# Seven block products for eight in the gated branch and the output projection, over all 1024 tokens

## Chip, cores and metric

The kernel runs on one core of one Trainium2 chip. The metric is the device time of one launch in microseconds; the median of three runs counts. Everything is float32.

## What is computed

One decoder layer on x (1 x 1024 x 2048), then a final modulated norm:

```python
mod = c_act @ w_ada + b_ada                  # shift, scale, gate
h = modulate(rms_norm(x, norm_g), shift, scale)
proj = h @ w_in                              # 2048 x 5632
u_a, v_a, z_a, q, k, v, z_b = split(proj)    # 1024, 1024, 1024, 1024, 256, 256, 1024
y_a = chunked_spatial_gating(u_a, v_a, ...)  # u * (W_s LN(v) + b), chunks of 128 tokens
y_b = sliding_window_sink_attention(rope(q), rope(k), v, sinks)   # window 128
y = concat([y_a * silu(z_a), y_b * silu(z_b)])
x = x + gate * (y @ w_out)                   # 2048 x 2048
out = modulate(rms_norm(x, final_norm_g), shift_f, scale_f)
```

## The kernel before

The tokens are worked in two halves of 512. Every large product is taken in float32 accuracy from three matmuls on rounded operands: an operand is split into a high part (a copy on ScalarE, rounded) and a low part (the rest, a subtraction on VectorE or GpSimd), and `mm3` (L199) sums high x high, high x low, low x high in PSUM. `split_w` (L138) splits weights as they come; h is split once per half and kept in SBUF as 16 pairs of 128x512 tiles (`Hh`, `Hl`, one pair per 128 rows of the contraction, called kt).

`project` (L250) makes one group of 512 output columns: 16 steps (kt), each with four 128x512 outputs, so 16 x 4 x 3 = 192 matmuls of 512 columns. There are eleven groups: u0, u1, kv, q0, q1, va0, va1, zb0, zb1, za0, za1. The order of half 0 is: va0 and va1 on the unnormalised x, while `mod_col` (L155) makes the scale column; kv and q0 while it makes the shift column and `build_h` (L494) makes h; then `half` (L744): q1, zb0, zb1, u0, u1, za0, za1, and the output projection `out_phase` (L543). Half 1 builds its h during the end of half 0's output projection and runs kv, q0, q1, va0, va1, zb0, zb1, u0, u1, za0, za1 and the output projection.

Beside the projections run three kinds of work. `side` holds generators (attention, then the spatial sums of the gating branch); `tick` (L230) lets them advance by `credit` steps per kt. `bg` holds column work: `mod_col` takes two loads of 128x1024 of w_ada and two multiply-reduces on VectorE per column of 128 values (gate, final scale and shift: 96 of them), and `corr_bg` 16 similar blocks; `background(n)` advances it by n, and `background(1000)` empties it. The order on each engine is set by a scheduler when the kernel is built: program order with priorities (`tc.high_priority`). All loads and stores but one go through SyncE's queue, in order.

```python
mm3(o, lh, ll, rh, rl)    # o += lh.T rh + lh.T rl + ll.T rh
```

## Time and profile before

| what | us |
|---|---|
| runs, median (lowest to highest of 3) | 1536.05 (1533.2 to 1536.28) |
| profiled execution, span | 1539.1 |
| TensorE busy | 1461.2 (95%) |
| VectorE busy | 1000.6 (65%) |
| ScalarE busy | 630.8 (41%) |
| GpSimd busy | 253.6 (16%) |

The profiled execution is one execution of its own; the profile gives its span, 0.2% above the median of the runs, and no other time for it. A busy share is an average over stages; a row of matmuls gives their modelled length, while the distance between their starts is what one costs.

### The profile page before, as it was taken

How to read it: one execution, taken by the hardware profiler on the slowest of the kernel's cores; microseconds unless marked ns; L12 is line 12 of the kernel's file. 1: busy time of each engine (PE TensorE's matmuls, PEld its weight loads, DVE VectorE, ACT ScalarE, POOL GpSimd, SP SyncE). 2: the span in 40 equal slices, each digit the busy share in tenths (PEclk: the TensorE clock that was granted, in tenths of full speed). 3: DMA queues.
4: the chain of work that ended last, by engine and by line, in shares of the span. 5: the costliest groups of instructions: out<-in, count | busy, mean ns of one | idle time of the engine just before them, and what ended most of it. 6: DMA issues, size and time to landing. Idle time of an engine off the chain costs nothing.

```text
span 1539.1 us, 20360 instructions
## 1 busy us (share of the span) xinstructions
PE 1461.2 (95%) x7057; PEld 1213.1 (79%) x7057; DVE 1000.6 (65%) x1952; ACT 630.8 (41%) x1397; POOL 253.6 (16%) x183
## 2 busy tenths in 40 slices
...
GB/s 348 282 203 267 270 190 140 153 175 195 109 111 121 198 200 219 205 220 187 144 184 244 181 195 157 123 125 141 120 186 175 205 203 196 171 219 197 133 87 110
DMA packets 88106, 280.65 MB, mean 182 GB/s; under 512 B 12017, under 2 KB 12609, under 8 KB 88002
## 3 DMA queue, kind: packets, MB, share of 16 engines
...
q10 hardware_dynamic: 144, 0.52, 0.1%
...
## 4 chain that ended last, share of the span: by engine, by line
PE 43%; issue 28%; DVE 14%; DMA 9%; ACT 2%; POOL 2%; SPq 0%; DVEq 0%; ACTq 0%; POOLq 0%
PE mm L200 11%; PE mm L202 11%; PE mm L201 11%; DMA ring<-ada 4%; DVE ring L165 3%; DMA wr<-ada 1%; PE att L202 1%; PE att L201 1%; PE att L200 1%; DVE wl L149 1%; PE att L349 1%; DVE ring L720 1%; DVE y L165 1%; DMA ring<-wvaT 1%; DVE t L333 1%
## 5 line engine op out<-in xcount | busy, mean ns | idle before, releaser
L202 PE MATMUL mm<-r,wl 128*128 128x512 f32 x1024 | 403.5, 394 | 4.9 <-DVE wl L149 3.8
L200 PE MATMUL mm<-r,wh 128*128 128x512 f32 x1024 | 405.5, 396 | 0.8 <-ACT wh L148 0.4
L201 PE MATMUL mm<-r,wh 128*128 128x512 f32 x1024 | 403.4, 394 | 0.0
L148 ACT ACTIVATE wh<-wr 128x512 fp32r<-128x512 f32 x318 | 197.6, 627 | 335.5 <-PE mm L201 192.0
L149 DVE TENSOR_TENSOR wl<-wr,wh 128x512 fp32r<-128x512 f32 x226 | 163.8, 729 | 132.6 <-ACT wh L148 127.4
L202 PEld LDWEIGHTS mm<-r,wl 128*128 128x128 f32 x1024 | 194.5, 190 | 49.1 <-DVE wl L149 6.8
L200 PEld LDWEIGHTS mm<-r,wh 128*128 128x128 f32 x1024 | 195.3, 191 | 40.5 <-ACT y L279 1.2
L201 PEld LDWEIGHTS mm<-r,wh 128*128 128x128 f32 x1024 | 195.0, 190 | 37.8
L200 PE MATMUL mm<-wh,r 128*128 128x512 f32 (+1 forms) x448 | 171.4, 383 | 18.3 <-ACT r L656 16.0
L201 PE MATMUL mm<-wl,r 128*128 128x512 f32 (+1 forms) x448 | 170.9, 381 | 3.1 <-POOL wl L149 2.5
L148 ACT ACTIVATE wh<-ring 128x512 fp32r<-128x512 f32 x138 | 86.8, 629 | 207.7 <-PE mm L201 124.7
L149 POOL TENSOR_TENSOR wl<-wr,wh 128x512 fp32r<-128x512 f32 x92 | 130.5, 1420 | 228.4 <-ACT wh L148 209.7
L202 PE MATMUL mm<-wh,r 128*128 128x512 f32 (+1 forms) x448 | 166.7, 379 | 0.1
L201 PE MATMUL att<-wl,r 128*128 128x512 f32 (+1 forms) x448 | 161.7, 361 | 2.0 <-DVE wl L149 1.9
L200 PE MATMUL att<-wh,r 128*128 128x512 f32 (+1 forms) x448 | 161.0, 359 | 0.0
L202 PE MATMUL att<-wh,r 128*128 128x512 f32 (+1 forms) x448 | 161.0, 359 | 0.0
L149 DVE TENSOR_TENSOR wl<-ring,wh 128x512 fp32r<-128x512 f32 x138 | 97.7, 711 | 95.7 <-ACT wh L148 87.9
L200 PEld LDWEIGHTS mm<-wh,r 128*128 128x128 f32 x448 | 85.6, 191 | 38.5 <-ACT r L656 21.0
L474 POOL TENSOR_TENSOR y<-y,t 128x512 f32<-128x512 f32 x32 | 47.7, 1515 | 394.1 <-ACT t L483 349.3
L201 PEld LDWEIGHTS mm<-wl,r 128*128 128x128 f32 x448 | 85.8, 191 | 20.7 <-POOL wl L149 5.4
L201 PEld LDWEIGHTS att<-wl,r 128*128 128x128 f32 x448 | 84.7, 189 | 18.1 <-DVE wl L149 4.6
L202 PEld LDWEIGHTS mm<-wh,r 128*128 128x128 f32 x448 | 85.5, 191 | 16.0 <-DVE r L657 0.8
(213 smaller groups left out, 2033.4 us busy)
## 6 DMA issues: line engine op xcount, KB each, us to landing
wr<-win SPq DMA_DIRECT2D x124, 512.0 KB, 4.2
ring<-ada SPq DMA_DIRECT2D x90, 512.0 KB, 5.2
wr<-ada SPq DMA_DIRECT2D x55, 512.0 KB, 4.4
ring<-win SPq DMA_DIRECT2D x46, 512.0 KB, 3.9
wr<-wout SPq DMA_DIRECT2D x38, 512.0 KB, 3.6
ring<-wout SPq DMA_DIRECT2D x26, 512.0 KB, 3.9
ring<-wvaT SPq DMA_DIRECT2D x16, 512.0 KB, 5.3
y<-xn SPq DMA_DIRECT2D x16, 512.0 KB, 4.8
```

Of the source, the lines that this page charges most:

```text
L148: act.activation(R(w_hi[i]), r[:, kk, :], AF.Copy)
L149: (pool if on_pool else dve).tensor_tensor(R(w_lo[i]), r[:, kk, :], w_hi[i], op=ALU.subtract)
L165: dve.tensor_tensor_reduce(w, w, cb[:, c0:c0 + n], scale=1.0, scalar=prev, op0=ALU.mult, op1=ALU.add, accum_out=o)
L200: pe.matmul(o, lhsT=lh, rhs=rh, start=first, stop=False)
L201: pe.matmul(o, lhsT=lh, rhs=rl, start=False, stop=False)
L202: pe.matmul(o, lhsT=ll, rhs=rh, start=False, stop=last)
L333: dve.tensor_tensor_reduce(ps[i], os[i], mk, scale=-0.125, scalar=nsnk[:, h0 + i:h0 + i + 1], op0=ALU.add, op1=ALU.min, accum_out=nm[:, i: ...
L349: pe.transpose(pt_bank[:, c:c + P], p[:, 256 * i + P * j:256 * i + P * j + P], ident)
L474: pool.tensor_tensor(y, y, zz[c], op=ALU.mult)
L720: dve.tensor_tensor_reduce(ti, ti, misc, scale=1.0, scalar=prev, op0=ALU.mult, op1=ALU.add, accum_out=acc_)
```

## The change

u, za and the output projection leave `half`. They become eight *units* behind both halves: u, za, and the two column halves o0 and o1 of the output projection, each twice (c = 0, 1: the two halves of the contraction). A unit multiplies a 1024 x 1024 block of tokens and features by a 1024 x 1024 block of weights, both cut in 2 x 2, with seven products of 512 x 512 x 512 instead of eight. One product is 48 matmuls of 512 columns. For that the tokens' side needs seven operands (`SUMS`: blocks, sums and differences), built by `op_make` from h or y in DRAM and split in high and low; the weights' side needs four sums, made on GpSimd (`w_sums` and two more in `unit`). Results are added on VectorE from PSUM, and a first visit (c = 0) leaves its four partial results in DRAM (`part_d`) for the second.

h, y, v, the gating sums and u therefore go through DRAM (`h_d`, `y_d`, `v_d`, `s_d`, `us_d`). va of both halves comes first, one group over all 1024 tokens at a time (eight PSUM banks); weights of va are read once. The scale loop now holds va0, the shift loop va1, and kv and q0 follow alone. Half 1 does q0 before kv. Buffers come from three pools (`Arena`): `al2` gives 128x1024, `al` half of one, first free first.

```diff
+    def al2(self):
+        if not self.big:
+            raise MemoryError(f"{len(self.half)} halves left")
+        return self.big.popleft()
+
+    def al(self):
+        if not self.half:
+            self.half.extend(self.of[id(self.al2())][1])
+        return self.half.popleft()
+
+    def fr(self, t):
+        b, other = self.of[id(t)]
+        if b is t:
+            self.big.append(t)
+        elif any(x is other for x in self.half):
+            self.half = deque(x for x in self.half if x is not other)
+            self.big.append(b)
+        else:
+            self.half.append(t)
...
+    lend(both, 2, "w", NW)
+    lend(both, 1, "r", NR)
+    lend(both, 0, "f", NF)
+    front_r = lend(front, 1, "fr", NB - NW - NR - NF)
+    cb = [al2(), al2()]
...
+    def build_h(h, kt, rb):
+        x, hi, lo = al(), al(1), al(1)
+        sp.dma_start(out=x, in_=A["xT"][h, kt])
+        dve.scalar_tensor_tensor(x, x, scale_c[:, kt:kt + 1], rb, op0=ALU.mult, op1=ALU.mult)
+        act.activation(x, x, AF.Identity, bias=shift_c[:, kt:kt + 1])
+        sp.dma_start(out=h_d[h, kt], in_=x)
+        act.activation(R(hi), x, AF.Copy)
+        dve.tensor_tensor(R(lo), x, hi, op=ALU.subtract)
+        fr(x)
+        H[kt] = hi, lo
...
+    def w_load(u, b):
+        name, c = u
+        wts[b] = [al2() for _ in range(2)]
+        for jj in range(2):
+            sp.dma_start(out=two(wts[b][jj]), in_=A["ww"][PAIRS.index(name), c, BLOCKS.index(b), jj])
+
+    def w_sums():
+        wts["t2"] = [al2() for _ in range(2)]
+        for jj in range(2):
+            t3, t2 = wts["12"][jj], wts["t2"][jj]
+            pool.tensor_tensor(t3, wts["22"][jj], t3, op=ALU.subtract)
+            pool.tensor_tensor(t2, t3, wts["11"][jj], op=ALU.add)
+
+    def product(op, w, bank, feature, refill, first):
+        for jj in range(2):
+            hi, lo = al2(2), al2(2)
+            act.activation(R(hi), wts[w][jj], AF.Copy)
+            dve.tensor_tensor(R(lo), wts[w][jj], hi, op=ALU.subtract)
+            ah, al_ = ops[op][jj]
+            for i in range(2):
+                for s in range(4):
+                    n, m = slice(512 * i, 512 * i + 512), slice(512 * i + s * P, 512 * i + s * P + P)
+                    x, y = ((hi, lo), (ah, al_)) if feature else ((ah, al_), (hi, lo))
+                    mm3(bank[s], R(x[0])[:, m], R(x[1])[:, m], R(y[0])[:, n], R(y[1])[:, n],
+                        first and jj + i == 0, jj + i == 2, not first)
+            fr(hi, lo)
+        while stale:
+            op_make(*stale.pop())
+        if refill:
+            stale.append((op, *refill))
...
+    SUMS = {"11": ["11"], "s2": ["21", "22", "-11"], "12": ["12"], "s3": ["11", "-21"], "s1": ["21", "22"], "22": ["22"],
+            "s4": ["12", "11", "-21", "-22"]}
+
+    def op_make(name, src, kind, c):
+        if name in ops:
+            for t in ops.pop(name):
+                fr(*t)
+        made = []
+        for jj in range(2):
+            total = None
+            for b in SUMS[name]:
+                t = al2()
+                rows_ = ROWS[kind][c][int(b[-1]) - 1]
+                sp.dma_start(out=two(t), in_=src[int(b[-2]) - 1, rows_[2 * jj]:rows_[2 * jj] + 2].rearrange("k p t -> p k t"))
+                if total is None:
+                    total = t
+                else:
+                    dve.tensor_tensor(total, total, t, op=ALU.subtract if b[0] == "-" else ALU.add)
+                    fr(t)
+            hi, lo = al2(1), al2(1)
+            act.activation(R(hi), total, AF.Copy)
+            dve.tensor_tensor(R(lo), total, hi, op=ALU.subtract)
+            fr(total)
+            made.append((hi, lo))
+        ops[name] = made
...
+        w_load(u, "21")
+        product("11", "11", X, feature, refill, True)
+        p1 = [al() for _ in range(4)]
+        evac(lambda s: act.activation(p1[s], X[s], AF.Copy))
+        for jj in range(2):
+            pool.tensor_tensor(wts["11"][jj], wts["22"][jj], wts["t2"][jj], op=ALU.subtract)
+        if c:
+            u2, u3, c21 = past(1), past(3), past(2)
+            for t in (u2, u3, c21):
+                for s in range(4):
+                    pool.tensor_tensor(t[s], t[s], p1[s], op=ALU.add)
+            fr(*p1)
+            c11 = past(0)
+        hk(0)
+        product("s2", "t2", Y, feature, refill, True)
+        if c == 0:
+            u2 = [al() for _ in range(4)]
+            add(u2, Y, p1)
         else:
...
+            add(u2, Y, u2)
+        hk(1)
+        product("12", "21", X, feature, refill, False)
...
+            add(c11, X, c11)
+        leave(0, c11)
+        for jj in range(2):
+            pool.tensor_tensor(wts["21"][jj], wts["21"][jj], wts["t2"][jj], op=ALU.subtract)
+        fr(*wts.pop("t2"))
+        hk(2)
+        product("s3", "12", Y, feature, refill, False)
+        if c == 0:
+            u3 = [al() for _ in range(4)]
+            add(u3, Y, p1)
+        else:
+            add(u3, Y, u3)
+        fr(*wts.pop("12"))
+        w11 = wts.pop("11")
+        if nxt:
+            w_load(nxt, "11")
+        n11 = wts.pop("11", None)
+        wts["11"] = w11
+        hk(3)
+        product("s1", "11", X, feature, refill, True)
+        add(u3, X, u3)
+        leave(3, u3)
+        fr(*wts.pop("11"))
...
+            wts["11"] = n11
+            w_load(nxt, "12")
...
+        product("22", "21", Y, feature, refill, False)
...
+        add(c21, Y, c21)
+        leave(2, c21)
+        fr(*wts.pop("21"))
+        w22 = wts.pop("22")
+        if nxt:
+            w_load(nxt, "22")
...
+    for kt in range(KT):
...
+        a = scale_c[:, kt:kt + 1]
+        for _ in mod_col("scale", kt, a):
             pass
...
+        if kt % 2 == 0:
+            wr = chunk(A["win"][GI["va0"], kt // 2])
         dve.tensor_tensor(a, a, cols[:, C_G + kt:C_G + kt + 1], op=ALU.mult)
-        act.activation(R(Hh[kt]), X[kt], AF.Copy, scale=a)
-        dve.scalar_tensor_tensor(R(Hl[kt]), X[kt], a, Hh[kt], op0=ALU.mult, op1=ALU.subtract)
-        if kt == 0:
-            act.activation(acc, X[kt], AF.Square)
-        else:
-            q = sq[kt % 2]
-            act.activation(q, X[kt], AF.Square)
-            pool.tensor_tensor(acc, acc, q, op=ALU.add)
-
-    vb = project(["va0", "va1"], ["mm", "att"], per_kt=g1_kt, pool_lo=("va0",),
-                 steps=[(kt, g) for kt in range(KT - 2) for g in ("va0", "va1")]
-                 + [(kt, g) for g in ("va0", "va1") for kt in (KT - 2, KT - 1)])
-    raws, rings = deque(w_raw), deque(ring)
-
...
+        for h in range(2):
+            x, hi, lo = al(), al(1), al(1)
+            sp.dma_start(out=x, in_=A["xT"][h, kt])
+            act.activation(R(hi), x, AF.Copy, scale=a)
+            dve.scalar_tensor_tensor(R(lo), x, a, hi, op0=ALU.mult, op1=ALU.subtract)
+            XA[h, kt] = hi, lo
+            if kt == 0:
+                act.activation(acc[h], x, AF.Square)
+            else:
+                q = al()
+                act.activation(q, x, AF.Square)
+                pool.tensor_tensor(acc[h], acc[h], q, op=ALU.add)
+                fr(q)
+            fr(x)
+        W = split_w(halves(wr)[kt % 2], on_pool=True)
+        if kt % 2:
+            fr(wr)
+        for T in range(8):
+            va_mm(T, kt, W)
+        fr(*W)
+
...
+    order = [(kt, T) for kt in range(2) for T in range(2, 8)] + ["spread"] + [(kt, T) for kt in range(2) for T in range(2)]
+    order += [(kt, T) for kt in range(2, KT) for T in range(8)]
...
+        kt, T = step
+        if kt not in va1:
+            for _ in mod_col("shift", kt, shift_c[:, kt:kt + 1]):
+                pass
+            if kt % 2 == 0:
+                wr = chunk(A["win"][GI["va1"], kt // 2])
+            va1[kt] = split_w(halves(wr)[kt % 2], on_pool=True)
...
+        if not left[kt]:
+            fr(*va1[kt], *XA.pop((0, kt)), *XA.pop((1, kt)))
+            if kt > 0:
+                for k in ([0, 1] if kt == 1 else [kt]):
+                    build_h(0, k, rb[0])
+    va_out(1)
+    arenas[1].drop(front_r)
+    front.close()
+    lend(heads, 0, "hf", NB - NW - NR - NF)
+
+    kq = project(["kv", "q0"], ["att", "mm"], pool_lo=("q0",))
...
         def start(kt):
-            if kt == 6:
-                credit[0], credit[1] = 0.0, (0.74 if h == 0 else 0.58)
-
-        q1 = project(["q1"], ["mm"], bgn=(0, 1) if h else (1,), after_kt=start)["q1"]
+            if kt == 4:
+                credit[0], credit[1] = 0.0, 0.88
+
+        bgn = (1,)
+        q1 = project(["q1"], ["mm"], bgn=bgn, after_kt=start, pool_lo=("q1",))["q1"]
         q_grab(q1, (2, 3))
-        if h:
-            for i, g in enumerate(("va0", "va1")):
-                ps = project([g], ["mm"], bgn=(0, 1))[g]
-                for t in range(4):
-                    grab(Y[t][:, i, :], ps[t])
-        silu_gate(project(["zb0"], ["mm"], bgn=(0, 1) if h else (1, 1, 1, 1, 1, 1, 2, 1))["zb0"], 4, 16)
+        ps = project(["zb0"], ["mm"], bgn=bgn, pool_lo=("zb0",))["zb0"]
+        silu_gate(ps, h, 0, 16)
+        if h == 0:
+            while len(bg) > 1:
+                background(1)
         ln = norm_v(h)
 
...
+        def last(kt):
+            fr(*H.pop(kt))
+            next(ln, None)
+
+        ps = project(["zb1"], ["mm"], bgn=bgn, after_kt=last, pool_lo=("zb1",))["zb1"]
         for _ in ln:
             pass
-        silu_gate(zb1, 6, 32)
-        held = [rings.popleft(), rings.popleft()]
-        wr = prep_spatial(h, held)
-        side.append(spatial(*wr))
-        ps = project(["u0"], ["mm"], bgn=(h,))["u0"]
+        silu_gate(ps, h, 2, 32)
+        side.append(spatial(h))
         drain()
-        rings.extend(held)
...
+    bg.append(corr_bg())
+    bg.append(gate_bg())
     half(0, kq)
-
+    background(1000)
+    for kt in range(KT):
+        build_h(1, kt, rb[1])
+    fr(*rb)
...
+    kq = project(["q0"], ["mm"], bgn=(1,), pool_lo=("q0",))
+    kq.update(project(["kv"], ["att"], bgn=(1,)))
     half(1, kq)
+    background(1000)
+    fr(*cb, *K1, *K2, *V, *kprev, *pring, *tt)
+    heads.close()
+    both.close()
+    arenas[:] = [Arena(), Arena(), Arena()]
+    last_ = ctx.enter_context(ExitStack())
+    lend(last_, 2, "t", 4)
+    lend(last_, 1, "o", 28)
+    lend(last_, 0, "g", NB - 32)
+
+
+
+    UNITS = [("u", 0), ("za", 0), ("u", 1), ("za", 1), ("o0", 0), ("o1", 0), ("o0", 1), ("o1", 1)]
+    for b in ("11", "12", "22"):
+        w_load(UNITS[0], b)
+    w_sums()
+    for n in SUMS:
+        op_make(n, h_d, "h", 0)
...
+    def z_final(q, s, t):
+        h, f = q // 2, 4 * (q % 2) + s
+        m = al()
+        sp.dma_start(out=m, in_=us_d[h, f])
+        act.activation(t, t, AF.Silu)
+        pool.tensor_tensor(t, t, m, op=ALU.mult)
+        sp.dma_start(out=y_d[h, f], in_=t)
+        fr(m, t)
...
+        def final(q, s, t):
+            T, c = 4 * (q // 2) + s, 2 * g + q % 2
+            x = al()
+            sp.dma_start(out=x, in_=A["xn"][T][:, 512 * c:512 * c + 512])
+            dve.tensor_tensor(t, t, rows["g", q % 2], op=ALU.mult)
+            pool.tensor_tensor(t, t, x, op=ALU.add)
+            act.activation(x, t, AF.Square, accum_out=ssq[:, 4 * T + c:4 * T + c + 1])
+            dve.tensor_tensor(t, t, rows["a", q % 2], op=ALU.mult)
...
+    for k, u in enumerate(UNITS):
+        name, c = u
+        nxt = UNITS[k + 1] if k + 1 < len(UNITS) else None
+        refill = {1: (h_d, "h", 1), 3: (y_d, "y", 0), 5: (y_d, "y", 1)}.get(k)
+        final = {("u", 1): u_final, ("za", 1): z_final, ("o0", 1): o_final(0), ("o1", 1): o_final(1)}.get(u)
+        hook = o_hook(int(name[1])) if u in (("o0", 1), ("o1", 1)) else None
+        unit(u, k, nxt, refill, final, hook)
```

Three places in the order of the instructions, as the build prints them (engine's row: line, operation, written <- read, size; f, hf, t, g, wr, ring are SBUF buffers with their numbers, *_d are in DRAM).

SyncE's queue where half 1's h is loaded, before (L830 loads a block of x, L135 weights):

```order
L135 DMA wr1_91<-wout 128x1024
L135 DMA wr2_92<-wout 128x1024
L830 DMA t12_135<-xT 128x512
L830 DMA t13_136<-xT 128x512
L830 DMA t2_125<-xT 128x512
L830 DMA t11_134<-xT 128x512
L830 DMA t4_127<-xT 128x512
L135 DMA ring0_93<-wout 128x1024
L830 DMA t5_128<-xT 128x512
L830 DMA t12_135<-xT 128x512
```

and now (L292 loads a block of x, L295 stores the finished h block, L181 loads for a column, L167 weights):

```order
L295 DMA h_d_153<-f16_143 128x512
L181 DMA f11_138<-ada 128x1024
L167 DMA f2_129<-win 128x1024
L292 DMA f16_143<-xT 128x512
L181 DMA f15_142<-ada 128x1024
L167 DMA hf0_1489<-win 128x1024
L181 DMA f6_133<-ada 128x1024
L295 DMA h_d_153<-f16_143 128x512
L167 DMA f7_134<-win 128x1024
L181 DMA f12_139<-ada 128x1024
L292 DMA f16_143<-xT 128x512
```

The blocks of half 1 went into different buffers, t12, t13, t2 and so on, and now all go into one, f16 (all 16 of them in its second half), with a store of each between two loads.

VectorE between the spatial sums of half 0 and the h blocks of half 1, now (L183 is the multiply-reduce of a column, L293 scales a block of x, L297 makes the low part):

```order
L183 ISA f6_133,pc_s2_258<-f6_133,f0_127,cols_71 128x1024
L183 ISA pc_s2_258 128x1
L183 ISA f7_134,gate_c_81<-f7_134,f1_128,pc_s2_258 128x1024
L183 ISA gate_c_81 128x1
L183 ISA f12_139,pc_s3_301<-f12_139,f0_127,cols_71 128x1024
L183 ISA pc_s3_301 128x1
L183 ISA f17_144,gate_c_81<-f17_144,f1_128,pc_s3_301 128x1024
L183 ISA gate_c_81 128x1
L293 SCALAR_TENSOR_TENSOR f16_143<-f16_143,scale_c_79,f3_130 128x512
L297 TENSOR_TENSOR r3_99<-f16_143,r26_122 128x512
L183 ISA f8_135,pc_s0_174<-f8_135,f0_127,cols_71 128x1024
L183 ISA pc_s0_174 128x1
```

Nineteen such multiply-reduces (two rows each, the second reads the accumulator) stand in a row behind the last spatial sum and ahead of the scaling of the second h block (L293); before, the columns stood among the output projection's work. At the end of half 1 stand 18 in the same way.

SyncE's queue where the units begin, now (L181 column loads, L536 weight blocks, L577 blocks of h):

```order
L181 DMA hf0_1489<-ada 128x1024
L181 DMA f9_136<-ada 128x1024
L181 DMA f13_140<-ada 128x1024
L181 DMA f15_142<-ada 128x1024
L181 DMA f10_137<-ada 128x1024
L536 DMA g0_6833<-ww 128x1024
L205 DMA rows_d_152<-row_s0_2172 16x128
L536 DMA g1_6834<-ww 128x1024
L536 DMA g2_6835<-ww 128x1024
L536 DMA g3_6836<-ww 128x1024
L536 DMA g4_6837<-ww 128x1024
L536 DMA g5_6838<-ww 128x1024
```

The first weight block goes into g0, which lies where a buffer of the last multiply-reduce lay. Six weight blocks and 28 blocks of h follow before the weights of the unit's third product. On TensorE 2688 matmuls of 128x512 (L213 to L215) follow each other from there to the end; 3072 did the same work before.

## Rows read from the trace of the kernel before

**Rows 1.** The page: busy time of each engine, and what the DMA moved.

```profile
PE 1461.2 (95%) x7057; PEld 1213.1 (79%) x7057; DVE 1000.6 (65%) x1952; ACT 630.8 (41%) x1397; POOL 253.6 (16%) x183
...
DMA packets 88106, 280.65 MB, mean 182 GB/s; under 512 B 12017, under 2 KB 12609, under 8 KB 88002
```

**Rows 2.** Busy time by stage; columns in the first line, after start:end and length.

```profile
core 0: us, PE busy (x) PEld busy (x) DVE busy (x) ACT busy (x) POOL busy (x), PEclk, DMA share, GB/s
0.00:113.00 113.00, 91.95 (x360) 68.69 (x361) 93.23 (x121) 41.75 (x69) 44.43 (x34) 1.00 0.76 276
...
113.00:121.00 8.00, 7.64 (x41) 6.04 (x41) 5.48 (x14) 4.34 (x9) 2.07 (x1) 1.00 0.97 371
121.00:217.00 96.00, 90.48 (x476) 75.08 (x475) 78.59 (x111) 31.72 (x54) 23.18 (x16) 1.00 0.78 262
217.00:485.00 268.00, 241.55 (x1204) 199.64 (x1203) 197.39 (x509) 146.23 (x401) 117.14 (x85) 0.95 0.47 140
485.00:617.00 132.00, 131.38 (x578) 108.16 (x577) 72.98 (x110) 42.35 (x70) 6.49 (x4) 1.00 0.59 196
617.00:802.00 185.00, 181.08 (x790) 148.03 (x789) 88.67 (x142) 68.02 (x126) 7.05 (x5) 0.99 0.58 186
802.00:891.00 89.00, 86.72 (x470) 74.50 (x469) 54.10 (x87) 29.14 (x53) 4.90 (x3) 1.00 0.70 223
891.00:1217.00 326.00, 319.31 (x1602) 268.77 (x1601) 234.05 (x573) 167.03 (x424) 27.60 (x20) 0.99 0.49 153
1217.00:1348.00 131.00, 131.00 (x580) 108.47 (x579) 65.00 (x99) 41.44 (x70) 5.49 (x4) 1.00 0.60 194
1348.00:1539.00 191.00, 180.08 (x970) 155.74 (x969) 111.10 (x194) 58.74 (x128) 15.25 (x12) 0.99 0.45 150
```

**Rows 3.** ScalarE's timeline: evacuation of u0 and of za1 of half 1.

```profile
1217.53 1.96 ACT L279 ACTIVATE y<-mm 128x512 f32<-128x512 f32 x3 [0.28 <-PE mm L202]
...
1348.24 1.28 ACT L483 ACTIVATE t<-mm 128x512 f32<-128x512 f32 x2 [0.27 <-PE mm L202]
```

**Rows 4.** Lines L165, L149, L498, L497, L513: min/median/max ns, first and last start.

```profile
L165 DVE CUSTOM_DVE_ANT_0 ring<-ring,cb,cols x48: 1272/1284/2372, 8.5 to 1276.9; 128x1024 f32<-128x1024 f32 x48
L165 DVE CUSTOM_DVE_ANT_0 ring<-ring,cb,pc_s x43: 751/1284/2356, 9.9 to 1285.1; 128x1024 f32<-128x1024 f32 x41, 128x512 f32<-128x512 f32 x2
...
L149 DVE TENSOR_TENSOR wl<-wr,wh x226: 675/689/1780, 11.7 to 1475.9; 128x512 fp32r<-128x512 f32 x113
...
L149 POOL TENSOR_TENSOR wl<-wr,wh x92: 1262/1310/2263, 27.3 to 478.1; 128x512 fp32r<-128x512 f32 x92
...
L498 DVE SCALAR_TENSOR_TENSOR r<-t,shift_c,r x24: 739/748/753, 121.6 to 817.4; 128x512 fp32r<-128x512 f32 x24
...
L497 ACT ACTIVATE r<-t,shift_c x24: 712/724/727, 120.8 to 816.7; 128x512 fp32r<-128x512 f32 x24
...
L513 DVE TENSOR_TENSOR t<-mm,t x12: 424/684/686, 712.1 to 1505.3; 128x512 f32<-128x512 f32 x10, 128x256 f32<-128x256 f32 x2
```

**Rows 5.** Timeline of VectorE and GpSimd during rope, 221 to 227: start, duration.

```profile
221.20 1.73 POOL L283 TENSOR_TENSOR t<-y,t 128x512 f32<-128x512 f32 x1
221.71 1.77 DVE L282 TENSOR_TENSOR t<-y,t 128x512 f32<-128x512 f32 x1
223.01 1.62 POOL L286 TENSOR_TENSOR y<-y,t 128x512 f32<-128x512 f32 x1
...
227.13 1.41 DVE L285 TENSOR_TENSOR t<-y,t 128x512 f32<-128x512 f32 x1
```

**Rows 6.** The chain of waits, 800 to 813; DMA issues: KB each, median us to landing.

```profile
802.89 4.14 DMA t<-xT
...
809.46 2.50 DMA t<-xT
...
t<-xT SPq DMA_DIRECT2D x24, 256.0 KB, 5.3
...
x_d<-y SPq DMA_DIRECT2D x8, 512.0 KB, 5.3
...
ring<-x_d SPq DMA_DIRECT2D x4, 512.0 KB, 4.4
...
out<-y SPq DMA_DIRECT2D x4, 256.0 KB, 2.6
```

745 lines of the change are left out of this document (342 added, 403 removed).

## Prediction

> **What bounds the kernel now.** I read the page's busy shares first, then the busy time stage by stage, then TensorE's pace inside one stage, last what each wait is for. TensorE is busy for 95% of the span, and the DMA moves 182 GB/s on average [rows 1]. The stages show where the other 5% lie [rows 2]: the three projections u1, za0, za1 of the second half (1217 to 1348) have TensorE busy without a gap, while the first loop (0 to 113) and the attention stage of the first half (217 to 485) leave it idle 21 and 26 us. So nearly everything hides under matmuls, and the change has to be judged by what it does to that cover as much as by the matmuls it saves.
>
> The pace: 576 matmuls lie between the evacuation of u0 at 1217.53 and that of za1 at 1348.24 [rows 3]: 130.7/576 = 0.227 us each, 43.6 us for a group of 192. Before there are 2 x (11 x 192 + 768) = 5760 of this size. The change turns 3072 of them (u, za, output projection) into 8 units x 7 products x 48 = 2688. The saving is 384 x 0.227 = **87 us**. Everything below is set against that.
>
> **The change, stage by stage.** The stages of before add up to its span: 113 + 104 + 268 + 132 + 185 + 89 + 326 + 131 + 191 = 1539 [rows 2]. I rebuild the span from the stages of the changed order.
>
> *First loop (va0 for all 1024 tokens, with the scale column).* A step keeps 24 matmuls (5.4 us), but its VectorE and GpSimd work grows. A 1024-wide multiply-reduce takes 1.28 us on VectorE, plus 0.08 for its accumulator; a two-input op on 512 columns 0.69 to 0.75 there and 1.31 on GpSimd [rows 4]. Where both engines have such ops, neither keeps that pace: between 221 and 227 each VectorE op takes 1.4 to 1.8 and each GpSimd op 1.6 to 1.7, and a pair starts every 1.7 us [rows 5], against 0.69 + 1.31 = 2.0 for the two added up. So the two engines' times nearly add, at 0.85 of the sum. Before, a step had two multiply-reduces (2.73), one h split (0.75), one weight split on VectorE (0.69), two ops on GpSimd (2.62): 6.8, and took 100/16 = 6.3 (0.92 of the sum). Now: 2.73 + 2 x 0.75 + 3 x 1.31 = 8.2. At 0.85 to 0.92 that is 6.9 to 7.5; I take 7.3, 16 x 7.3 + 13 us of start = 130 (ends 122 and 138).
>
> The Trainium skill (SBUF — State Buffer, section "Who interferes with whom") has it stricter: a VectorE op with two SBUF inputs and a GpSimd op that reads SBUF exclude each other for the whole instruction. By that the loop takes 16 x 8.2 + 13 = 144 and the sum below is 14 us more here; the rows just named overlap by 15%, so the measurement is taken, and the rule is the second rival.
>
> *Second loop (va1, shift column, h of half 0).* Matmuls 5.4 us a step, VectorE plus GpSimd 2.73 + 0.75 + 0.69 + 1.31 = 5.5. The like loop of before took 96/16 = 6.0 [rows 2] with 0.75 more on VectorE. I take 5.8: 93, plus the 8 us handover that 113 to 121 shows: 101 (96 to 106). *kv and q0 of half 0* then run without such work: the 89 us that they take in half 1 now.
>
> *Rest of half 0 (q1, zb0, zb1, attention, spatial).* Before, 268 us for these and u0 [rows 2]. u0's matmuls leave (43.6), the rest stays, and attention has one group less to hide under: 268 - 43.6 + 6 = 230 (222 to 245).
>
> *First seam.* What is left of the gate columns is now issued behind the spatial sums: 19 multiply-reduces stand on VectorE before the second h block can be scaled, each with its own 512 KB load. 19 x (1.28 + 0.08 + 0.05) = 27 us (23 to 30). Nothing covers it: TensorE's next work is q0, which needs those h blocks. Before, such columns ran under u, za and the output projection.
>
> *h of half 1.* All 16 blocks go through one and the same 128x512 buffer: the next load waits until the previous block has been stored to DRAM. That is a chain of load, scale, shift, store. Scale 0.75, shift 0.72 [rows 4], two issues of 0.33. For load and store no row shows this pattern; the ends are the fastest transfers, 2.5 us for a load of xT and 2.6 for a store of this size, and the medians 5.3 and 5.3 [rows 6]. A link is 7.2 to 12.7 us; I take 3.3 each way (mean of the 4.14 and 2.50 of two xT loads in such company [rows 6]), 8.7. Fourteen links behind the seam: 122, plus 5 for the last block's matmuls: **127** (105 to 185), where q0 has 43.6 us of matmuls. The loss is 83. Before, up to 14 buffers served these blocks, the output projection ran meanwhile, and nothing had to be stored.
>
> The Trainium skill (DMA: Bandwidth & Descriptors, section "Anatomy of one DMA — SWDGE (gpsimd) path") fits a DMA on the GpSimd queue as 2.0 us plus bytes over 436 GB/s; that estimate is 2.6 us for 256 KB, and 108 instead of 127 here, 1681 in the end. The two fastest transfers agree with it, the medians of this SP queue do not.
>
> *kv* 89/2 = 45. *Rest of half 1:* 326 us minus va0, va1, u0 (3 x 43.6), plus 5 for the lost cover: 200 (195 to 212).
>
> *Second seam.* 18 multiply-reduces of the last columns (25 us), on whose buffer the first weight block of the units waits; then eight blocks of 512 KB, at the 371 GB/s of the best stretch [rows 2] 11 us, and 4 for landing and the first split: 40 (33 to 46).
>
> *The units.* 2688 x 0.227 = 610. Losses: (a) in unit 1 the third product's weights are queued behind 34 blocks; 36 x 0.524 MB / 371 GB/s = 51, landed at 53, and TensorE is there 37 us after the first issue (15 + two products of 10.9): about 18. (b) The engines' sum per unit of 76 us: weight splits 14 x 1.22 on VectorE (1.28 less 0.53 for 512 columns gives the slope) and 8 weight sums on GpSimd (2.5 each, at most twice 1.31): 37. Second visits add 12 sums and 16 closing multiplies on GpSimd: 36. Rebuilding the seven operands adds 28 x 1.22 = 34. The fourth unit has all three: 107, at 0.85 91 us. It also has about two free buffers for 28 loads of 4.4 us [rows 6] and 1.2 of use: 28 x 5.6/2 = 78. I take 30 lost there. (c) Elsewhere sums of 71 to 95 at 0.85 lie near 76; waits of some 5 us in each of six units: 30. Together **80** (30 to 180). VectorE's additions from PSUM (0.68) fit in the rest.
>
> *End.* Four row tiles are closed behind the last product instead of the one now (191 us for 174 of matmuls, [rows 2]): 25 (18 to 40).
>
> **Sum:** 130 + 101 + 89 + 230 + 27 + 127 + 45 + 200 + 40 + 610 + 80 + 25 = 1704, against 1539.1 of the profiled execution. The runs' median is 3 us below that span, so I predict **1700**: 165 above before. Saved are 87 on products; lost some 170 at the two seams and in the h chain, and 80 in the units.
>
> **Rivals.** (1) *The units keep TensorE's pace* but for (a): the scheduler's order is early enough that splits and operand rebuilds hide. For it: sums at 0.85 fit in seven of eight units. Against: rebuild and split share VectorE's one queue, and a late load blocks both. 1704 - 60: 1640.
> (2) *VectorE and GpSimd times add in full.* First loop +14, fourth unit +16, seventh (95 against 81) +14, last +12: 1760. The 15% overlap in [rows 5] speaks against it; with a queue blocked at each product it reaches 1800. It is the rule of SBUF — State Buffer in the Trainium skill.
> (3) *Faster: the loads run ahead.* If column loads, h blocks and unit operands are all issued so early that VectorE never meets one that hasn't landed, the waits of 27 + 83 + 40 + 80 = 230 us fall away and 1704 becomes 1474, the runs 1470. It decides from the point where less than 65 of the 230 are left. Against it: one buffer for 16 blocks, the last column op in front of the first weight block, and queues whose order no timing changes.
> (4) *The saving isn't there*: the instruction count says it is. TensorE's lower level could eat some of it (the granted clock averages 0.95 in the first half's attention stage, where it waits often [rows 2]); that lands in (2).
>
> **How the numbers follow.** Forecast (1660 to 1750) 0.55, (1) 0.20, (2) 0.18, (3) 0.05, a draw 0.02. A measurement tells about 0.2%, 3 us, from nothing. Faster 0.05, same 0.02, slower 0.93. The range takes in (1) and (2) and the middle of the bounds: the link alone spans 80 us, the unit losses 150. 1600 to 1815.
>
> **What would show it.** Right: TensorE nearly idle for 20 to 30 us behind the first half's spatial sums, then bursts of 12 matmuls every 8 to 9 us for over 100 us, the chain of waits alternating h load, VectorE, ScalarE and h store; another idle 40 before the first product; the fourth unit the longest, near 105, GpSimd and VectorE ops stretched there. Wrong: q0 of half 1 in under 60 us, or units at 76 us throughout.

## The result, and the profile after

The changed kernel takes **1860.74 us** (median of 4, 1856.22 to 1865.49), the kernel before 1534.62 in the same comparison: ratio **1.213** (95% interval 1.210 to 1.216). Slower was right; 1700 and the range up to 1815 were too low. The loss is 326 us, forecast were 165.

The page of the kernel after: busy time of each engine, and two groups, VectorE's low parts of weights in the units (L549) and GpSimd's in the projections (L173).

```profile
PE 1475.1 (79%) x6521; PEld 1184.8 (64%) x6521; DVE 1240.2 (67%) x1916; ACT 652.4 (35%) x1299; POOL 725.6 (39%) x432
...
L173 POOL TENSOR_TENSOR w<-f,w 128x512 fp32r<-128x512 f32 x148 | 227.3, 1545 | 514.4 <-ACT w L172 476.9
...
L549 DVE TENSOR_TENSOR t<-g,t 128x1024 fp32r<-128x1024 f32 x112 | 168.2, 1506 | 110.7 <-ACT t L548 110.4
```

Against [rows 1], TensorE is 79% busy instead of 95%, GpSimd's time has nearly tripled, VectorE has 240 us more. A low part of 1024 columns, estimated at 1.22 us, takes 1.51 on average, and one of 512 on GpSimd 1.55 where [rows 4] have a median of 1.31.

Busy time by stage of the kernel after, columns as in [rows 2]: first loop, second loop with the handover, kv and q0, rest of half 0, first seam, q0 of half 1 on its h chain, kv, rest of half 1, second seam; then the eight units and the tail. Four rows are left out: kv and q0 (250 to 338), kv (738 to 788), the second seam (1011.6 to 1057.3) and the sixth unit (1532.8 to 1612.3).

```profile
0.00:131.50 131.50, 102.64 (x370) 74.34 (x371) 105.77 (x117) 50.14 (x85) 82.15 (x51) 0.95 0.70 240
131.50:250.00 118.50, 108.72 (x452) 86.37 (x452) 80.45 (x115) 37.52 (x61) 32.85 (x19) 0.93 0.81 280
...
338.00:580.60 242.60, 200.96 (x996) 164.08 (x996) 202.69 (x518) 129.99 (x373) 95.90 (x66) 0.93 0.52 169
580.60:616.00 35.40, 1.54 (x9) 1.06 (x9) 26.98 (x43) 1.48 (x4) 0.00 (x0) 0.57 0.83 310
616.00:738.00 122.00, 76.87 (x215) 53.90 (x216) 45.14 (x57) 29.18 (x46) 22.14 (x16) 0.73 0.58 196
...
788.00:1011.60 223.60, 200.97 (x1062) 166.17 (x1061) 176.49 (x460) 129.40 (x361) 89.36 (x65) 0.97 0.49 159
...
1057.30:1165.70 108.40, 84.24 (x337) 67.40 (x338) 71.71 (x61) 30.82 (x35) 33.98 (x12) 0.85 0.63 225
1165.70:1242.30 76.60, 76.46 (x337) 62.91 (x336) 56.56 (x52) 30.90 (x34) 21.52 (x9) 1.00 0.71 250
1242.30:1325.80 83.50, 78.94 (x337) 63.89 (x337) 54.22 (x49) 18.71 (x21) 54.52 (x29) 0.98 0.61 207
1325.80:1438.20 112.40, 85.03 (x338) 67.87 (x337) 65.85 (x57) 34.56 (x42) 57.48 (x37) 0.85 0.64 220
1438.20:1532.80 94.60, 80.65 (x338) 65.41 (x337) 49.63 (x46) 23.94 (x29) 40.74 (x17) 0.91 0.57 198
...
1612.30:1710.30 98.00, 82.49 (x338) 65.77 (x337) 72.65 (x70) 25.27 (x40) 56.34 (x30) 0.91 0.59 195
1710.30:1812.00 101.70, 85.46 (x336) 67.39 (x335) 71.40 (x82) 28.58 (x53) 57.13 (x37) 0.92 0.42 132
...
1812.00:1863.50 51.50, 0.00 (x0) 0.00 (x0) 27.92 (x40) 7.94 (x16) 20.00 (x17) 0.52 0.58 199
```

The saving is there: the second unit takes 76.6 us, seven products of 10.9. But only it and the sixth (79.5) come near that; the longest are the fourth and the first. The units are told apart by counting 336 matmuls for each on TensorE's timeline. One matmul of the eighth unit stands early, at 1697.86, ahead of the last 20 of the seventh, which therefore ends at 1710.3.

The shown busy times of VectorE and GpSimd add up to more than the unit in six of the eight, but an op that is held up counts as busy too. An estimate goes by undisturbed durations instead: 1.22 and 0.69 us on VectorE for 1024 and 512 columns, 2.4 and 1.3 on GpSimd, additions from PSUM left out. By it the fourth, seventh and eighth unit hold 95, 88 and 92 us of such work, against 76 of matmuls; the other five hold 61 to 78.

TensorE's timeline shows the two seams, and the first unit's wait ahead of its third product:

```profile
614.10 0.38 PE L202 MATMUL att<-ident,gate_c 128*16 128x128 f32 x1 [32.31 <-DVE gate_c L183]
...
1043.23 0.38 PE L202 MATMUL att<-ident,shf_c 128*16 128x128 f32 x1 [31.19 <-DVE shf_c L183]
1057.33 1.22 PE L213 MATMUL mm<-o,t 128*128 128x512 f32 x2 [13.72 <-ACT o L584]
...
1108.09 0.79 PE L213 MATMUL mm<-o,t 128*128 128x512 f32 x1 [20.40 <-ACT t L548]
```

The fourth unit's longest wait shows how the engines hang together. Its rows are from the timelines of TensorE, ScalarE and GpSimd; the last one is SyncE's waits from 1335 to 1372 (us in total, times, longest):

```profile
1369.58 0.80 PE L213 MATMUL att<-o,t 128*128 128x512 f32 x1 [16.40 <-ACT t L548]
...
1367.52 1.06 ACT L584 ACTIVATE o<-g 128x1024 fp32r<-128x1024 f32 x1 [24.36 <-DMA g<-y_d]
...
1351.55 14.71 POOL L633 TENSOR_TENSOR g<-g,g 128x512 f32<-128x512 f32 x12
...
SPq L577 <- POOL g L633: 11.3, 2, 9.4
```

TensorE waits 16.4 us for a split of weights on ScalarE (L548). ScalarE had stood 24.4 us in front of the op before that one, the split of a rebuilt operand (L584), which needs a block of y. SyncE issued the load of that block 9.4 us late, because the buffer for it came free only with one of GpSimd's sums of the second visit (L633).

And SyncE's queue shows the chain of half 1's h, here without the column and weight loads between:

```profile
617.92 0.33 SPq L292 DMA_DIRECT2D f<-xT  x1
625.32 0.33 SPq L295 DMA_DIRECT2D h_d<-f  x1
627.73 0.33 SPq L292 DMA_DIRECT2D f<-xT  x1
...
733.00 0.33 SPq L292 DMA_DIRECT2D f<-xT  x1
```

Load and store strictly alternate. From the load at 617.92 to that at 733.00 it is 13 links, 8.9 us each.

### The profile page after: what moved, and what is told of

The parts are those of the page before. It is cut to its first block, busy times and chain, and to the rows that moved or that the text cites. A ratio compares the mean times of both kernels' runs of the same rounds, so it can differ in the third digit from the quotient of the medians.

```text
span 1863.5 us, 19987 instructions
## 1 busy us (share of the span) xinstructions
PE 1475.1 (79%) x6521; PEld 1184.8 (64%) x6521; DVE 1240.2 (67%) x1916; ACT 652.4 (35%) x1299; POOL 725.6 (39%) x432
## 5 line engine op out<-in xcount | busy, mean ns | idle before, releaser
L173 POOL TENSOR_TENSOR w<-f,w 128x512 fp32r<-128x512 f32 x148 | 227.3, 1545 | 514.4 <-ACT w L172 476.9
L213 PE MATMUL mm<-r,w 128*128 128x512 f32 x512 | 214.0, 425 | 45.5 <-ACT r L296 42.2
L549 DVE TENSOR_TENSOR t<-g,t 128x1024 fp32r<-128x1024 f32 x112 | 168.2, 1506 | 110.7 <-ACT t L548 110.4
L214 PE MATMUL mm<-r,w 128*128 128x512 f32 x512 | 214.5, 419 | 0.7 <-DVE r L297 0.7
L215 PE MATMUL mm<-r,w 128*128 128x512 f32 x512 | 212.5, 415 | 2.1 <-POOL w L173 1.8
L548 ACT ACTIVATE t<-g 128x1024 fp32r<-128x1024 f32 x112 | 117.8, 1055 | 266.6 <-PE mm L214 76.4
L172 ACT ACTIVATE w<-f 128x512 fp32r<-128x512 f32 x178 | 109.3, 624 | 193.8 <-PE mm L214 86.0
L213 PEld LDWEIGHTS mm<-r,w 128*128 128x128 f32 x512 | 104.3, 205 | 71.8 <-ACT r L296 48.8
L183 DVE CUSTOM_DVE_ANT_0 f<-f,f,pc_s 128x1024 f32<-128x1024 f32 x77 | 119.6, 1559 | 36.0 <-DMA f<-ada 34.9
L183 DVE CUSTOM_DVE_ANT_0 f<-f,f,cols 128x1024 f32<-128x1024 f32 x76 | 121.3, 1601 | 32.5 <-DMA f<-ada 32.4
L215 PEld LDWEIGHTS mm<-r,w 128*128 128x128 f32 x512 | 104.3, 204 | 28.1 <-POOL w L173 5.1
L585 DVE TENSOR_TENSOR o<-g,o 128x1024 fp32r<-128x1024 f32 x56 | 87.9, 1580 | 48.4 <-ACT o L584 48.3
L214 PEld LDWEIGHTS mm<-r,w 128*128 128x128 f32 x512 | 104.5, 204 | 23.3 <-DVE r L297 3.9
L213 PE MATMUL mm<-o,t 128*128 128x512 f32 x224 | 91.0, 407 | 34.1 <-ACT t L548 20.4
L581 DVE TENSOR_TENSOR g<-g,g 128x1024 f32<-128x1024 f32 x56 | 87.4, 1573 | 41.8 <-DMA g<-y_d 33.7
L584 ACT ACTIVATE o<-g 128x1024 fp32r<-128x1024 f32 x56 | 58.8, 1056 | 156.6 <-DVE g L581 92.9
L213 PE MATMUL att<-o,t 128*128 128x512 f32 x224 | 90.1, 402 | 17.5 <-ACT t L548 17.5
L542 POOL TENSOR_TENSOR g<-g,g 128x1024 f32<-128x1024 f32 x16 | 43.6, 2726 | 147.7 <-DMA g<-ww 147.7
L215 PE MATMUL att<-o,t 128*128 128x512 f32 x224 | 90.5, 404 | 9.4 <-DVE t L549 9.4
L215 PE MATMUL mm<-o,t 128*128 128x512 f32 x224 | 91.1, 407 | 6.9 <-DVE t L549 6.8
```

The source lines that it names most:

```text
L172: act.activation(R(hi), src, AF.Copy)
L173: (pool if on_pool else dve).tensor_tensor(R(lo), src, hi, op=ALU.subtract)
L183: dve.tensor_tensor_reduce(t, t, cb[hf], scale=1.0, scalar=prev, op0=ALU.mult, op1=ALU.add, accum_out=o)
L213: pe.matmul(o, lhsT=lh, rhs=rh, start=first, stop=False, skip_group_check=on)
L214: pe.matmul(o, lhsT=lh, rhs=rl, start=False, stop=False, skip_group_check=on)
L215: pe.matmul(o, lhsT=ll, rhs=rh, start=False, stop=last, skip_group_check=on)
```

## The experiments

Theory A: VectorE and GpSimd exclude each other, so that their times add up (rival 2 of the prediction); on top come waits for buffers and queues. Theory B: the engines run side by side, and the units wait for loads and for VectorE's own queue.

**The lock by itself.** A kernel with none of the layer's work:

```diff
+    for phase in ((sub,), (padd,), (sub, padd), (padd5,), (ttr, padd5), (stt, padd5), (padd_psum, padd5), (dcopy, padd), (acopy,), (acopy, padd)):
+        bar()
+        for i in range(16):
+            for f in phase:
+                f(i)
```

> A kernel of its own that computes nothing of the layer: 16 VectorE ops and 16 GpSimd ops on tiles of their own, alone and at once, in ten stretches with a barrier between. VectorE subtractions of 128x1024 alone 16 x 1.22 = 20 us, GpSimd additions alone 16 x 2.4 = 38, both at once: theory A (they exclude each other) 58 us, theory B (side by side) 38 to 45. 16 multiply-reduces of 128x1024 with 16 GpSimd additions of 128x512: A 16 x (1.28 + 0.08 + 1.3) = 43, B 22. VectorE additions with one input in PSUM, 16 x 0.68 = 11, with the same GpSimd additions, 21: no theory of mine says; A in its wide form 32, in its narrow form (only two inputs in SBUF) 21. ScalarE copies of 128x1024 beside GpSimd: 38 by both.

The timelines of VectorE and GpSimd in it. L53 is a subtraction of 128x1024 on VectorE, L65 a product of two tiles of 512 columns and a scalar, L68 an addition with one input in PSUM; L56 and L59 are GpSimd's additions of 1024 and 512 columns. What runs beside them: nothing at 70.50 and 160.22, VectorE's subtractions at 107.46, multiply-reduces at 179.94, L65 at 215.48, L68 at 242.48, VectorE's copies at 262.24, ScalarE's copies at 321.78.

```profile
52.05 18.25 DVE L53 TENSOR_TENSOR do<-a,b 128x1024 fp32r<-128x1024 f32 x16 [52.05 <-SPq L50]
107.42 50.41 DVE L53 TENSOR_TENSOR do<-a,b 128x1024 fp32r<-128x1024 f32 x16 [37.11 <-SPq L50]
...
215.45 26.86 DVE L65 SCALAR_TENSOR_TENSOR do<-a,acc,b 128x512 f32<-128x512 f32 x16 [1.27 <-SPq L50]
242.47 9.66 DVE L68 TENSOR_TENSOR do<-bank,b 128x512 f32<-128x512 f32 x16 [0.16 <-SPq L50]
...
70.50 36.77 POOL L56 TENSOR_TENSOR po<-c,d 128x1024 f32<-128x1024 f32 x16 [58.04 <-SPq L50]
107.46 52.57 POOL L56 TENSOR_TENSOR po<-c,d 128x1024 f32<-128x1024 f32 x16 [0.19 <-SPq L50]
160.22 19.54 POOL L59 TENSOR_TENSOR po<-c,d 128x512 f32<-128x512 f32 x16 [0.19 <-SPq L50]
179.94 35.35 POOL L59 TENSOR_TENSOR po<-c,d 128x512 f32<-128x512 f32 x16 [0.19 <-SPq L50]
215.48 26.29 POOL L59 TENSOR_TENSOR po<-c,d 128x512 f32<-128x512 f32 x16 [0.19 <-SPq L50]
242.48 19.57 POOL L59 TENSOR_TENSOR po<-c,d 128x512 f32<-128x512 f32 x16 [0.71 <-SPq L50]
262.24 44.03 POOL L56 TENSOR_TENSOR po<-c,d 128x1024 f32<-128x1024 f32 x16 [0.19 <-SPq L50]
321.78 36.88 POOL L56 TENSOR_TENSOR po<-c,d 128x1024 f32<-128x1024 f32 x16 [15.51 <-SPq L50]
```

Alone 18.25 and 36.77, at once 52.57: 96% of the sum 55.02. GpSimd's 16 additions of 512 columns take 19.54 alone, 35.35 beside multiply-reduces of 1024 columns, and 26.29 beside the products of L65, a pair every 1.68 us. They take 19.57 beside VectorE additions that read one input from PSUM, which themselves take 0.60 us each: no lock there. Beside VectorE copies of 1024 columns GpSimd's 36.77 become 44.03; beside ScalarE nothing changes (36.88). Theory A holds, in its narrow form: additions from PSUM, like those of the units (L602), are free of it, the three kinds of op with both inputs in SBUF are not. This is what the Trainium skill states (SBUF — State Buffer, section "Who interferes with whom"), down to the input in PSUM.

In the kernel after it looks like this (VectorE's low parts and GpSimd's ops in the eighth unit):

```profile
1720.78 3.26 DVE L549 TENSOR_TENSOR t<-g,t 128x1024 fp32r<-128x1024 f32 x1
...
1743.80 1.21 DVE L549 TENSOR_TENSOR t<-g,t 128x1024 fp32r<-128x1024 f32 x1
...
1720.27 2.69 POOL L628 TENSOR_TENSOR g<-g,g 128x1024 f32<-128x1024 f32 x1 [1.23 <-DVE t L549]
...
1743.84 3.41 POOL L652 TENSOR_TENSOR g<-g,g 128x1024 f32<-128x1024 f32 x1
...
1749.25 2.39 POOL L652 TENSOR_TENSOR g<-g,g 128x1024 f32<-128x1024 f32 x1
```

The low part of 1720.78 starts while GpSimd's op of 1720.27 runs and takes 2.05 us more than an undisturbed one; at 1743.80 VectorE was first by 0.04 us, and it is GpSimd that takes 1.02 more.

**GpSimd out of the units.**

```diff
-            pool.tensor_tensor(t3, wts["22"][jj], t3, op=ALU.subtract)
+            dve.tensor_tensor(t3, wts["22"][jj], t3, op=ALU.subtract)
...
-                    pool.tensor_tensor(t[s], t[s], p1[s], op=ALU.add)
+                    dve.tensor_tensor(t[s], t[s], p1[s], op=ALU.add)
```

> The 136 GpSimd ops of the eight units (weight sums, sums of second visits, closing multiplies and adds) go to VectorE; nothing else is changed. Theory A (the two engines exclude each other, so a unit takes about the sum of their own times, 105 us in the fourth and 114 in the last): an op that costs 1.3 or 2.4 us on GpSimd costs 0.69 or 1.22 on VectorE, the sums fall to 81 and 89, and below 76 in the six others. Fourth unit near 85, eighth near 92, units together 755 to about 690, total about 1795. Theory B (the engines run side by side and the units wait for loads and for VectorE's own queue): VectorE gets 12 to 28 us more in each unit and TensorE waits for its weight splits longer; units 755 to 800, total 1860 to 1905.

1802.32 us (ratio 1.175, 1.171 to 1.180), 58 below after: near theory A's number, and the opposite of B's sign. The stages of units and tail, and the group of low parts:

```profile
1051.20:1758.30 707.10, 635.73 (x2687) 516.52 (x2688) 542.74 (x630) 224.36 (x284) 1.46 (x2) 0.94 0.65 221
1758.30:1798.70 40.40, 0.41 (x2) 0.00 (x0) 28.79 (x55) 8.40 (x18) 4.37 (x6) 0.56 0.72 253
...
L549 DVE TENSOR_TENSOR t<-g,t 128x1024 fp32r<-128x1024 f32 x112 | 136.0, 1220 | 73.1 <-ACT t L548 73.1
```

The low part is back at 1.22 us; units 754.7 to 707.1, tail 51.5 to 40.4. The three units that hold more engine work than matmuls gain most: the fourth falls from 112.4 to 88.7, the seventh from 98.0 to 86.6, the eighth from 101.7 to 92.3 (the expectation's 114 for the last unit goes by a boundary at 1697.9); the fifth, behind the fourth, falls by 9. The third and the sixth become 4 and 6 us longer. The edit takes away two things at once, the lock and ops that last twice as long on GpSimd; what each is worth is not separated here.

**Low parts of projection weights on VectorE.**

```diff
-        (pool if on_pool else dve).tensor_tensor(R(lo), src, hi, op=ALU.subtract)
+        dve.tensor_tensor(R(lo), src, hi, op=ALU.subtract)
```

> All low parts of projection weights on VectorE; 148 of 178 were on GpSimd. Theory A: 1.31 us there become 0.69 here, 92 us less of summed time; the first loop (sum 129 of 131.5 us) falls to about 121, the rest of half 0 (sum 241 of 231) and of half 1 (237 of 222) by 10 to 20 each, total about 1820. Theory B: VectorE, busy 111 of 131 us in the first loop already, gets 11 us more there and 20 more in each half; nothing falls, total 1860 to 1890.

1816.87 (1.185, 1.174 to 1.196): 44 less, again A's number. The first loop takes 120 instead of 131.5; the last matmuls of half 0's spatial sums start at 555 instead of 581; half 1 from kv to its last spatial sum takes 276 instead of 286.

**Own buffers for h.**

```diff
-        x, hi, lo = al(), al(1), al(1)
+        xb, hi, lo = al2(), al(1), al(1)
+        x = halves(xb)[0]
...
-        fr(x)
+        fr(xb)
```

> The 16 blocks of half 1's h go through rotating buffers instead of one. If the chain load, scale, shift, store through one buffer sets the pace (8 us a block over 124 us): loads run ahead during the seam, the stretch from the first h block to the end of q0 falls from 124 to 50 to 60, total about 1795. If the order of SyncE's queue or the column loads between them set it: 100 to 124, total 1840 to 1860.

1804.39 (1.177, 1.173 to 1.180), 56 less. q0 now runs in 46.4 us without gaps. It starts 27 us after the gate row, though: its first weights stand in SyncE's queue behind the 16 blocks. From the last spatial sum to kv it is 107 us, 145 in after.

**Third weights first.**

```diff
-        w_load(u, "21")
+        if "21" not in wts:
+            w_load(u, "21")
...
-    for b in ("11", "12", "22"):
+    for b in ("11", "12", "22", "21"):
         w_load(UNITS[0], b)
```

> The weights of the first unit's third product are loaded with the first six blocks instead of behind 28 blocks of h. If their place in the queue makes TensorE wait 20.6 us ahead of the third product: first unit 108 to about 88, total about 1840. If the wait only moves (the operand blocks of the later products are two loads later, or VectorE's rebuild order is what is late): first unit 100 to 108, total 1852 to 1861.

The first unit takes 95.9 instead of 108.4, between the two cases. The total, 1851.72 (1.208, 1.203 to 1.212), can hardly be told from after. The third product still waits, and TensorE's and ScalarE's timelines show for what:

```profile
1100.65 0.80 PE L213 MATMUL mm<-o,t 128*128 128x512 f32 x1 [11.94 <-ACT g L627]
...
1098.11 2.00 ACT L584 ACTIVATE o<-g 128x1024 fp32r<-128x1024 f32 x2 [4.00 <-DVE g L581]
```

The wait of 20.4 us has become one of 11.9 for ScalarE's copy of the first product out of PSUM (L627). That copy comes right behind splits of operands (L584), which wait in ScalarE's queue for VectorE's sums (L581). So the second case describes what is left: the order in which the operands are built is late.

**The tail's buffers.**

```diff
-            x = al()
+            xb = al2() if g and q == 1 else None
+            x = halves(xb)[0] if g and q == 1 else al()
...
-                t = al()
+                t = halves(tb)[0] if T < 4 else al()
```

> The last four row tiles load x and their first results into buffers of their own instead of just freed halves. After is idle twice in the tail until a load lands (7.9 and 5.3 us on GpSimd), each issued only once an output store had freed its half. If the halves set the pace: the tail falls from 53 to about 35 us, total about 1843. If the chain of each tile (sum, power, scale, add) and the lock of the two engines set it: 48 to 53, total 1856 to 1861.

1853.26 (1.205, 1.202 to 1.209); tail 45.7 instead of 51.5. A third of what was expected: freed halves cost some 6 us there. The total is only just clear of after. e1's 11 us in the tail come with GpSimd's ops.

**Four together.** The edits of e1, e2, e3 and e5, and:

```diff
-    background(1000)
     for kt in range(KT):
         build_h(1, kt, rb[1])
+        background(2)
+    background(1000)
```

> Units without GpSimd, all low parts on VectorE, h blocks in their own buffers, third weights first, together, and the columns left at the first seam issued between the h blocks (two per block). If the four are separate costs they add: 1861 - 58 - 44 - 56 - 9 = 1694, and the first seam's 33 us now lie beside q0's matmuls: about 1665. If they cover one another (VectorE, with all of GpSimd's work, becomes the bound of both halves and the units): 1710 to 1740.

1718.02 (1.117, 1.108 to 1.127): 143 less where the four alone give 168, and nothing of the first seam. TensorE now idles 55 us in front of the transposition of the gate row, which stands in its queue ahead of q0 and waits for the last column. Issued beside the h blocks, the columns still end before q0 can start.

**Columns in the halves.** As f1, with:

```diff
-        bgn = (1,)
+        bgn = (2,) if h else (1, 2)
```

and the tail's buffers.

> The one before, with half again as many columns in half 0 and twice as many in half 1 per step (so that none are left at the seams), and the tail's own buffers. If TensorE sets the pace of the halves, the columns hide there: second seam 46 to about 18, tail 40 to 30, total some 35 below the one before. If VectorE sets it (half 1 has 197 busy of 222 us), 24 columns of 1.36 us only move from the seam into the half: total within 15 of the one before. Theory that the change can win at all: under 1535; by my sums it can't, 1620 to 1660.

1691.01 (1.100, 1.097 to 1.103), 27 below f1. The second seam falls from 50 to 20, but the first half ends 18 later. From the first half's last spatial sum to q0 it is still 48 us, and SyncE's queue and TensorE show why:

```profile
613.92 0.42 SPq L167 DMA_DIRECT2D f<-win  x1
...
620.23 0.80 PE L213 MATMUL mm<-r,w 128*128 128x512 f32 x1 [17.47 <-ACT w L172]
```

q0's first weights are issued at 613.92, behind all loads of h.

**Columns early, alone on the kernel after.**

```diff
+    bg.append(gate_bg())
...
-    kq = project(["kv", "q0"], ["att", "mm"], pool_lo=("q0",))
+    kq = project(["kv", "q0"], ["att", "mm"], bgn=(3,), pool_lo=("q0",))
...
+            background(1000)
+            bg.append(final_bg())
```

> Only the place of the columns: gate columns from kv, q0 of half 0 on (three per step of two kt, where VectorE is busy 28 of 100 us), scale and shift of the final norm from zb1 of half 0 on; none stands at the first seam any more. If a column costs only where nothing covers it: first seam 33 to about 3, second 46 to 35, nothing given back; total about 1825. If VectorE's time is short everywhere, the columns are given back in kv and q0 of half 0 and in the halves: total 1845 to 1861.

1814.72 (1.184, 1.179 to 1.189), 46 less. TensorE goes from the last spatial sum to q0 within 1 us, and the second seam falls from 46 to 38. Columns cost only where nothing covers them.

**h stores on another queue.**

```diff
-        sp.dma_start(out=h_d[h, kt], in_=x)
+        act.dma_start(out=h_d[h, kt], in_=x)
```

> The stores of h go out on ScalarE's queue instead of SyncE's; nothing else. If in SyncE's queue they hold up the loads behind them (second loop: weights issued 6.4 us behind the store that waits for ScalarE, TensorE waits 1 to 4 us every second kt): second loop 118 to about 108, the one-buffer chain of half 1 shorter by the issue, 110 to 104; total about 1845. If the landing of the stores and the buffers set both: no change, 1855 to 1863.

1848.90 (1.206, 1.203 to 1.210): 12 less. From the first store of v to that of the second loop it is 103 us instead of 112, so half of the 17 that the second loop exceeded its forecast is loads waiting in line behind stores. The h chain of half 1 keeps its pace.

**Interleaved, and the last version of this line.** As f3 without its columns in the halves, with g0's, and:

```diff
+    kq = project(["q0"], ["mm"], bgn=(2,), pool_lo=("q0",), after_kt=lambda kt: kt + 3 < KT and build_h(1, kt + 3, rb[1]))
```

> As f3_all, but with the columns placed as in g0 and the h blocks of half 1 written between q0's steps, so that q0's weights no longer stand in SyncE's queue behind 16 block loads and stores and no gate row stands in TensorE's queue before q0. f3_all idles TensorE 48 us from the last spatial sum to q0, 20 at the second seam. If order of queues is what is left there: 48 to about 12, halves lighter by some 10, total about 1645. If VectorE's total (columns, low parts, former GpSimd work) is the bound: 1675 to 1690.

1666.80 (1.087, 1.085 to 1.090), between the two cases: from the last spatial sum of half 0 to kv it is 62 us instead of f3's 94, so 32 of the 50 are gone by which that stretch was longer than q0's own matmuls (43.6).

The last one adds h stores on ScalarE's queue and moves the sums of second visits behind `product("s2", ...)`:

> As g1, with the sums of second visits on VectorE behind the second product's weight splits instead of ahead of them (third unit 89 us where its second product waits 10; seventh alike), and h stores on ScalarE's queue. About 10 in the third unit, up to 10 in the seventh and eighth, 10 in the second loop: some 25 below g1, 1620. To beat the kernel before it would need 110 more, which no stall left would give: units 694 for 610 of matmuls, halves 238 and 226, tail 35.

**1635.77** (1.066, 1.063 to 1.069): 225 of the change's 326 us are undone, with all of its products as they were. 101 remain.

**Operands built once.**

```diff
-        refill = {1: (h_d, "h", 1), 3: (y_d, "y", 0), 5: (y_d, "y", 1)}.get(k)
+        refill = None
```

> After, but the seven operands of the tokens' side are built once; the three rebuilds (second, fourth and sixth unit, working into the next) are left out, with their 84 loads and their sums and splits, so the units multiply stale operands. If the rebuilds hold the units: third unit 83 to 78, fourth 112 to about 85, fifth 95 to 77, seventh and eighth 200 to 185; units together 753 to about 690. If they hide and the weights' side (loads, sums, splits) sets the units: 735 to 753.

One execution of this kernel, which multiplies stale operands, takes 1802.85 us. The units:

```profile
1058.20:1748.00 689.80, 629.97 (x2685) 514.00 (x2686) 382.58 (x376) 182.93 (x241) 327.83 (x174) 0.95 0.48 162
```

754.7 becomes 689.8, as expected. The third and fifth unit now take 76.1 and 76.2 (83.5 and 94.6 in after), the fourth 85.3 (112.4). So the rebuilds, their loads, sums and splits together, hold 65 of the 145 us that the units take over their matmuls' 610. The first unit (108.0) is not touched by it, the seventh and the eighth hardly (93.2 and 98.6, where after has 98.0 and 101.7).

**Keeping TensorE busy in the second seam.**

```diff
+    for i in range(180):
+        pe.matmul(banks8["mm"][i % 4], lhsT=R(kprev[0])[:, :P], rhs=R(kprev[0])[:, :512], start=True, stop=True)
```

> After, with 180 matmuls of 512 columns more, whose result is not used, on TensorE during the second seam, where it has nothing to do for 46 us. If the first unit starts at the lower clock because of the stall: its first product falls from 14.6 to 10.9 us, its third, which follows another stall, stays at 14.1; total 4 below after. If the start of the unit is slow for another reason (operands landing one by one): 13 to 15 us again.

One execution, 1861.36: nothing gained, the first product takes 15.1 us. TensorE's timeline, and the busy times of two stretches, with the granted clock behind the brackets:

```profile
1011.35 40.16 PE L923 MATMUL mm<-r 128*128 128x512 f32 x176
1056.96 1.22 PE L213 MATMUL mm<-o,t 128*128 128x512 f32 x2 [5.34 <-ACT o L584]
1059.90 0.80 PE L214 MATMUL mm<-o,t 128*128 128x512 f32 x1 [1.72 <-DVE o L585]
...
1011.40:1051.00 39.60, 39.60 (x177) 32.82 (x176) 26.41 (x42) 1.06 (x1) 0.00 (x0) 1.00 0.73 263
1056.90:1063.00 6.10, 4.32 (x9) 3.00 (x10) 6.06 (x2) 1.07 (x2) 6.02 (x3) 0.50 1.05 408
```

The matmuls added run at 40.16/176 = 0.228 us until 1051.5. After the 5.3 us of idle that are left the granted clock is at 0.50, the lower of its two levels, and the next eight matmuls start 0.43 apart, until 1063. Such a restart costs 8 x 0.2 = 1.6 us; another 1.7 of the 4.2 by which this first product exceeds 10.9 is a wait for VectorE's low part of an operand (L585).

**The kernel before without GpSimd's low parts.** The same edit as in e2, in `split_w` (L149) of the kernel before.

> The kernel before with all low parts of weights on VectorE; 92 of them, all before 480 us, were on GpSimd. Theory A: the summed time of both engines in its first 485 us falls from 475 to about 418 us; TensorE is idle 21 us in its first loop and 26 in its attention stage of half 0, and half of that comes back: 1510 to 1522. If the low parts on GpSimd ran beside VectorE: VectorE gets 63 us more in 485, where it is busy 413; 1535 to 1560.

**1508.28 us** (five runs, 1505.63 to 1510.02), ratio **0.982** (0.981 to 0.984): 1.8% faster than the kernel before, and a little better than expected. Its attention stage of half 0 (from the evacuation of q0 to that of u0):

```profile
206.00:455.00 249.00, 231.90 (x1202) 192.75 (x1201) 202.50 (x572) 146.09 (x399) 28.98 (x21) 0.99 0.50 151
```

The attention stage, 268 us in [rows 2], takes 249, GpSimd 29 there instead of 117, and VectorE, with more ops, is hardly busier (202.5 against 197.4). u0 ends at 455 instead of 485. As in e1, the lock and GpSimd's longer ops go together.

## Why the prediction was wrong, step by step

| stage | forecast | measured |
|---|---|---|
| first loop | 130 | 131.5 |
| second loop | 101 | 118.5 |
| kv, q0 of half 0 | 89 | 88 |
| rest of half 0 | 230 | 242.6 |
| first seam | 27 | 35.4 |
| h chain of half 1 with q0 | 127 | 122 |
| kv | 45 | 50 |
| rest of half 1 | 200 | 223.6 |
| second seam | 40 | 45.7 |
| units | 690 | 754.7 |
| tail | 25 | 51.5 |
| sum | 1704 | 1863.5 |

Forecast were 1704 for the profiled execution, measured are 1863.5: 160 us are missing. The order of the stages and what each waits for came out; what failed are terms of the sum.

**Right.** The saving of 87 was there. The h chain takes 122 of 127 us, with links of 8.9 where 8.7 was forecast, and e3 shows that it is the buffer. In the first seam VectorE's multiply-reduces take 27.0 us, as forecast; the rest of its 35.4 is mostly waits for their loads (6.9). The second seam came out close. e3 gives back 56 of the 83 that the chain was to cost, g0 the first seam and 8 of the second. The first unit waits for its third weights, and the fourth is the longest, 112.4 where "near 105" was said. Rival 1 (units at TensorE's pace) and rival 3 (loads run ahead) did not happen; rival 2, at 1760 to 1800, was too low as well.

**The units, 65 of the 160.** The step that failed is "Elsewhere sums of 71 to 95 at 0.85 lie near 76; waits of some 5 us in each of six units". By unit, in us:

| unit | 1 | 2 | 3 | 4 | 5 | 6 | 7 | 8 |
|---|---|---|---|---|---|---|---|---|
| after | 108.4 | 76.6 | 83.5 | 112.4 | 94.6 | 79.5 | 98.0 | 101.7 |
| e1, without GpSimd | 102.7 | 78.1 | 87.7 | 88.7 | 85.8 | 85.2 | 86.6 | 92.3 |
| k2, without rebuilds | 108.0 | 76.2 | 76.1 | 85.3 | 76.2 | 76.2 | 93.2 | 98.6 |

Over 76.2 the first unit loses 32, forecast were 18; the fourth 36, forecast were 30. The other six were to lose 30 together and lose 77. The seventh and eighth lose 22 and 26, together 47; e1 gives 21 of that back, k2 8. The rebuilds stretch into the units behind them: what the third and fifth lose, 7 and 18, is all gone in k2. The waits fall on one place: in the units TensorE waits some 100 us for splits of weights (L548, L549), which stand in the queues of ScalarE and VectorE behind work that waits for something else. Five us a unit was too small a price for that.

**TensorE's lower level**, put at nothing in the sum and left to rival 4. In the units of the kernel after, 126 matmuls start 0.43 us after the one before, in some fifteen runs behind waits (the rows of the units have a mean granted clock of 0.85 to 1.00); at 0.227 they would take 25 us less. A single restart is cheap (k1, under 2 us), and a shorter wait would save it too, so this is a price of the waits and not a cause beside them. How much of the 25 the units would get back without it is not shown.

**The factor 0.85** did not fail. At the prices that the prediction used, the pairs in the kernel with nothing else in it come to 0.88 of the sum (3.29 us against 1.22 + 2.5), 0.83 (2.21 against 1.36 + 1.31) and 0.82 (1.68 against 0.75 + 1.31). The first loop, priced with it, took 131.5 us, where 130 was forecast; the full sum at the same prices gave 144. What the factor hides is that the engines do exclude each other: against undisturbed ops from start to start (18.25/16 = 1.14, 36.77/16 = 2.30) the overlap of the 1024-column pair is 4%. A good part of the 15% is in the form of the rows, since an op's shown duration overlaps that of the next on its own engine (1.14 from start to start, where 1.21 is shown for one), so sums of shown durations are too long even without a second engine.

**The rest of half 1, 24 missing.** The step is "326 us minus va0, va1, u0, plus 5". It took half 1 as it was, but `pool_lo` now sends the low parts of q1, zb0 and zb1 to GpSimd in both halves; before, GpSimd had 27.6 us in that stage [rows 2], after it has 89. The diff showed it; the sum has no term for it. e2 gives 10 of it back; what holds the other 14 is open.

**The tail, 26 missing.** "Four row tiles are closed behind the last product" was taken from a tail that closes one. Here the tiles pass VectorE, GpSimd and ScalarE in turn, with loads between that go into buffers just freed: GpSimd waits 7.9 and 5.3 us for two of them. e1 takes 11 off, t1 6, all edits 17 (g3: 34.6).

**The second loop, 17.5 missing.** The sum of engine times was right (5.5 us a step, TensorE 5.4) and not the bound: weights queue in SyncE behind the h stores, which wait for ScalarE's shift (L294), 64 us in all in that loop. g4 gives back 9; e2, which takes the weights' low parts off GpSimd, 4 by the same marks, and both together (g3) 10.

**Open:** the 12.6 us of the rest of half 0, of which e2's edit gives back part, and what holds the 77 us over eight times 76.2 in g3's units (687). k2's 65 were measured with GpSimd still in the units, and the two edits were not run together.
